# The last two key blocks of stick-breaking attention in three high-and-low passes, with norms written in place

## The chip, the cores and the metric

The kernel runs on one core of one Trainium2 chip. The metric is the device time of one execution in microseconds, as the median of several runs.

## What is computed

The reference is one hybrid decoder layer over 528 tokens (16 learned meta tokens and 512 of the sequence) of width 2048, in float32. The part that matters here is the attention of 8 heads of 128 columns:

```python
q = _rmsnorm(q.reshape(b, L, N_ATTN_HEADS, HEAD_DIM), g_q[l])
k = _rmsnorm(k.reshape(b, L, N_ATTN_HEADS, HEAD_DIM), g_k[l])
...
z = einsum('bqhd,bkhd->bhqk', q_blk, k_ctx) / math.sqrt(HEAD_DIM)
causal = kpos[None, :] < qpos[:, None]
log_beta = jax.nn.log_sigmoid(z)
log_keep = jnp.where(causal, jax.nn.log_sigmoid(-z), 0.0)
log_pass = lax.cumsum(log_keep, axis=3, reverse=True) - log_keep
w = jnp.where(causal, jnp.exp(log_beta + log_pass), 0.0)
o = jnp.einsum('bhqk,bkhd->bqhd', w, v_ctx)
```

Beside it runs a gated short convolution over 1024 channels; then come an output projection with a residual, and a SwiGLU feed-forward block of width 5632.

## The kernel before

Everything is held transposed: channels (or keys) on the 128 partitions, tokens along the free axis. A large product is done as *high and low parts in three passes*: an operand is split into a rounded part (type F32R) and the remainder, and the product is high x high + high x low + low x high, each a pass of TensorE with F32R operands. `split(hi, lo, src)` (L323) makes the parts: a copy on ACT for the high part and a subtraction on DVE for the low part. Weights are loaded by DMA, split the same way (`split_quad`, L195) two pieces ahead of their use, and fed to `product` (L319). A product in plain F32 is a single call, but the profile shows it as two weight loads and two matmuls.

The eight heads come one after another (`head`, L514). For each head three products over the 16 blocks of the input give k (`pk`), q (`pq`) and v (`pv`) in PSUM, in passes of 256 and 272 columns for k and v, and of 512 for q. The smaller steps of a head are hung into the products of the next: `after(n, work)` (L290) holds a step until n blocks of the running products have been issued, and the framework then orders the instructions of each engine once, when the program is built. Each engine runs its own instructions in that order and waits at semaphores.

The steps of a head are these:

- `read_qk` (L405) reads k or q out of PSUM into a temporary `raw`. `qk_norm` (L489) sums the squares over the partitions with a matrix of ones (`ss_k`, `ss_q`, L501 and L502) and normalises by `rsqrt` (L326). The result goes to a tile of its own, `kn` (640 columns, of which 528 are tokens and the rest zeros) or `qn` (512). Then the high and low parts are made: `kh`, `kl` of the first 384 columns of `kn`, and `qh`, `ql` of all of `qn`.
- `attend` (L542) transposes v into PSUM (`ta` for the first four blocks of 128 keys, `tb` for the last 16). The first 384 columns are split into `vh`, `vl`; the last two blocks are copied into `v32` in F32. There are five key blocks: four of 128 keys and one of 16. The queries that a block has to meet begin at `Q0 = [0, 112, 240, 368, 496]`, so the logits of the blocks are 512, 400, 272, 144 and 16 queries wide. Blocks 0, 1 and 2 are done in three passes (L561 to L563), blocks 3 and 4 in F32 (L565, L566), into the columns of block 2's tile, so that there are three segments of 512, 400 and 432 columns.
- Per segment, ACT and DVE form softplus and log-sigmoid (`sp`, `lb`, L587 to L591), POOL masks (`causal`, L573), and `split` makes parts for the reverse cumulative sum, which is a product with a triangular matrix (`sums`, L610; `c`, L615 to L621). Segments are chained by one carry row: L626 and the split behind it. `sums` then forms the weights and splits them into `wh`, `wl`: all columns of segments 0 and 1, and the first 272 of segment 2.
- `mix` (L640) adds up the output `o`: blocks 0 to 2 in three passes (L645 to L647), block 3 in F32 with 128 rows (L648), block 4 in F32 with 16 rows (L649). Then `o` is scaled, split and sent to DRAM.

PSUM holds four small tiles (`small`, L66) in rotation, which the transposes, the logits, the sums and the outputs share. The temporaries with tag `e` (two of them) hold `raw` of k, `raw` of q and v in turn.

Of the kernel before, what the change touches and what calls it, by code (L numbers as in the profile page):

```python
# [9 lines left out]
F32 = mybir.dt.float32  # L10
F32R = mybir.dt.float32r
# [22 lines left out]
def hybrid_layer(ctx: ExitStack, tc: tile.TileContext, xT, w_in, w_out, w_gu, w_down, vecs, out):  # L34
# [288 lines left out]
    def split(hi, lo, src, eng=ve):  # L323
        return sc.copy(hi, src), eng.tensor_tensor(lo, src, hi.bitcast(F32), ALU.subtract)  # L324

    def rsqrt(dst, v, n, y=None, t=None, eng=ve, times=None):  # L326

        y = t512(n, "r", 3) if y is None else y
        t = t512(n, "r", 3) if t is None else t
        sc.activation(y[:, :n], v, AF.Ln)  # L330
        sc.activation(y[:, :n], y[:, :n], AF.Exp, scale=-0.5)
        last = sc.activation(t[:, :n], y[:, :n], AF.Square)
        if times is not None:
            eng.tensor_tensor(y[:, :n], y[:, :n], times, ALU.mult)
        eng.scalar_tensor_tensor(t[:, :n], t[:, :n], -0.5, v, ALU.mult, ALU.mult)
        eng.scalar_tensor_tensor(dst, t[:, :n], 1.5, y[:, :n], ALU.add, ALU.mult)
        return last
# [105 lines left out]


    apool = open_pool("apool", side="right")
    kns = [apool.tile([P, 640], F32, name=f"kn{i}") for i in range(1)]
    for t in kns:
        gp.memset(t[:, L:640], 0.0)
    for tag, n in (("kh", 384), ("kl", 384), ("sh", L), ("sl", L), ("qn", SEQ), ("qh", SEQ), ("ql", SEQ), ("bh", 288), ("bl", 288), ("sp", 1344)):
        apool.tile([P, n], F32 if tag in ("qn", "sp") else F32R, tag=tag, name=f"first_{tag}")  # L450
    accp.tile([P, 48], F32, name="pad_acc")
    acc_c = accp.tile([P, SEQ], F32, name="acc_c")
    acc_a = accp.tile([P, SEQ], F32, name="acc_a")
# [32 lines left out]
            split(st[:, :, 0], st[:, :, 1], x[:, m : m + 2])  # L486
            gp.dma_start(mix_dram[:, 2 - m : 4 - m, k], st.rearrange("p a b n -> p a (b n)"))

    def qk_norm(read, dst, parts_of, name):  # L489

        raw, s, cols = read[:3]
        sh = apool.tile([P, L], F32R, tag="sh", name=f"sh_{name}")[:, :cols]
        sl = apool.tile([P, L], F32R, tag="sl", name=f"sl_{name}")[:, :cols]
        cuts = [(0, cols)] if cols == SEQ else [(0, T2), (T2, L)]
        split(sh, sl, s)

        def finish():
            v = t512(L, "v", 2)[:, :cols]
            for a, b in cuts:
                q = small(f"ss_{name}{a}")[:, : b - a]  # L500
                pe.matmul(q, ones_r, sh[:, a:b], start=True, stop=False)  # L501
                pe.matmul(q, ones_r, sl[:, a:b], start=False, stop=True)  # L502
                ve.scalar_tensor_tensor(
                    v[:, a:b], q, 1.0 / P, eps_r2[:, L - cols + a : L - cols + b], ALU.mult, ALU.add
                )
            rsqrt(dst, v, cols, times=raw)
            hi, lo, n = parts_of
            split(hi, lo, dst[:, :n])

        return finish  # L510

# [2 lines left out]
    def head(h):  # L514

        if h:
            pk = pp.tile([P, 2, 512], F32, tag="pp", name=f"pk{h}")
            product(parts_of_all(pk), n_hl)
        read = read_qk(flat(pk), g_k, L) if h else read_k0
        kn = kns[0]  # L520
        kh = apool.tile([P, 384], F32R, tag="kh", name=f"kh{h}")
        kl = apool.tile([P, 384], F32R, tag="kl", name=f"kl{h}")
        after(8 if h else 19, qk_norm(read, kn[:, :L], (kh, kl, 384), f"k{h}"))

        if h:
            load_mix(h - 1)
            pq = pp.tile([P, 2, 512], F32, tag="pp", name=f"pq{h}")
            product([(pq[:, 0, :], META, L)], n_hl)
        read = read_qk(pq[:, 0, :], gq_s, SEQ) if h else read_q0
        qn = apool.tile([P, SEQ], F32, tag="qn", name=f"qn{h}")  # L530
        qh = apool.tile([P, SEQ], F32R, tag="qh", name=f"qh{h}")
        ql = apool.tile([P, SEQ], F32R, tag="ql", name=f"ql{h}")
        after(9 if h else 22, qk_norm(read, qn, (qh, ql, SEQ), f"q{h}"))

        pv = pp.tile([P, 2, 512], F32, tag="pp", name=f"pv{h}")
        product(parts_of_all(pv), n_hl)
        vt = t512(L, "e", 2)
        with tc.high_priority(0 if h else 1 << 20):
            ve.tensor_tensor(vt[:, :L], flat(pv), r, ALU.mult)
        after(6 if h else 15, lambda: attend(h, kn, kh, kl, qn, qh, ql, vt))  # L540

    def attend(h, kn, kh, kl, qn, qh, ql, vt):  # L542

        ta, tb = small(f"va{h}"), small(f"vb{h}")
        for b in range(4):
            pe.transpose(ta[:, b * P : (b + 1) * P], vt[:, b * P : (b + 1) * P], ident)
        pe.transpose(tb[:16, :P], vt[:, 512:L], ident)
        vh = apool.tile([P, 384], F32R, tag="vh", name=f"vh{h}")
        vl = apool.tile([P, 384], F32R, tag="vl", name=f"vl{h}")
        v32 = apool.tile([P, 256], F32, tag="v32", name=f"v32{h}")  # L550
        split(vh, vl, ta[:, :384])
        ve.tensor_copy(v32[:, :P], ta[:, 384:512])
        ve.tensor_copy(v32[:16, P:], tb[:16, :P])


        zs = {}
        for b in (2, 1, 0):
            zs[b] = z = small(f"z{h}_{b}")
            kk, q0 = slice(b * P, (b + 1) * P), Q0[b]
            n = SEQ - q0  # L560
            pe.matmul(z[:, :n], kh[:, kk], qh[:, q0:], start=True, stop=False)  # L561
            pe.matmul(z[:, :n], kh[:, kk], ql[:, q0:], start=False, stop=False)
            pe.matmul(z[:, :n], kl[:, kk], qh[:, q0:], start=False, stop=True)  # L563
            if b == 2:
                pe.matmul(z[:, 272:416], kn[:, 384:512], qn[:, 368:], start=True, stop=True)  # L565
                pe.matmul(z[:, 416:432], kn[:, 512:640], qn[:, 496:], start=True, stop=True)  # L566


        lw = apool.tile([P, 1344], F32, tag="lw", name=f"lw{h}")
# [40 lines left out]
        def sums(s):  # L610
            a, b = SEG[s]
            th, tl = hl[s]
            c = small(f"c{h}_{s}")
            if s == 2:
                pe.matmul(c[:, :432], later_r, th, start=True, stop=False)  # L615
                pe.matmul(c[:, :432], later_r, tl, start=False, stop=False)
                pe.matmul(c[:, P:416], ones_r, bh, start=False, stop=False)
                pe.matmul(c[:, P:416], ones_r, bl, start=False, stop=True)
            else:
                pe.matmul(c[:, : b - a], carry, th, start=True, stop=False)  # L620
                pe.matmul(c[:, : b - a], carry, tl, start=False, stop=True)  # L621
            if s:

                n, (a0, b0) = SEQ - Q0[s], SEG[s - 1]
                th, tl = hl[s - 1]
                ve.tensor_tensor(lw[0:1, b0 - n : b0], c[0:1, :n], sp[0:1, a : a + n], ALU.add)  # L626
                split(th[0:1, :], tl[0:1, :], lw[0:1, a0:b0])
                after(6, lambda: sums(s - 1))
            ve.tensor_tensor(lb[:, a:b], lb[:, a:b], c[:, : b - a], ALU.subtract)
            sc.activation(lw[:, a:b], lb[:, a:b], AF.Exp)  # L630
            causal(lw, s)
            n = (512, 400, 272)[s]
            th = apool.tile([P, b - a], F32R, tag=f"th{s}", name=f"wh{h}_{s}")
            tl = apool.tile([P, b - a], F32R, tag=f"tl{s}", name=f"wl{h}_{s}")
            split(th[:, :n], tl[:, :n], lw[:, a : a + n])
            ws[s] = (th[:, :n], tl[:, :n])
            if s == 0:
                after(11, lambda: mix(ws))

        def mix(ws):  # L640
            o = small(f"o{h}")
            for b in range(3):
                kk, q0 = slice(b * P, (b + 1) * P), Q0[b]
                th, tl = ws[b]
                pe.matmul(o[:, q0:], vh[:, kk], th, start=b == 0, stop=False)  # L645
                pe.matmul(o[:, q0:], vh[:, kk], tl, start=False, stop=False)
                pe.matmul(o[:, q0:], vl[:, kk], th, start=False, stop=False)  # L647
            pe.matmul(o[:, Q0[3] :], v32[:, :P], lw[:, 1184:1328], start=False, stop=False)  # L648
            pe.matmul(o[:, Q0[4] :], v32[:16, P:], lw[:16, 1328:1344], start=False, stop=True)  # L649
            g = g_att[:, h : h + 1]  # L650
            st = stage(f"st_o{h}")[:, : 2 * SEQ].rearrange("p (a b) -> p a b", a=2)
            hi = sc.activation(st[:, 0], o, AF.Copy, scale=g)
            lo = ve.scalar_tensor_tensor(st[:, 1], o, g, st[:, 0].bitcast(F32), ALU.mult, ALU.subtract)
            square_sum(acc_a, o, h == 0, eng=ve)
            gp.dma_start(oa_dram[h], st)
            if h < HEADS - 1:
                with tc.issue_after(hi.ins), tc.issue_after(lo.ins):
                    mix_x(h)
# [592 lines left out]
```

## Time and profile before

| what | value |
|---|---|
| median of three runs | 2037.42 us (2037.31 to 2037.79) |
| profiled execution, its own time | 2037.97 us |
| its span, first to last instruction | 2036.1 us |
| granted TensorE clock | 1.000 |
| attention of the eight heads | about 56 to 373 us of the span |
| instructions | 39674 |

The span is what the profile's views cover; the execution's own time is 1.87 us longer. In the views, PE is TensorE's matmul and PEld its weight load, DVE is VectorE, ACT is ScalarE, POOL is GpSimd. A row of the timeline gives start, duration, engine, line, operation and tiles (out<-in), then partitions x columns and a count. A row of the waits gives the waiting instruction, what it waited for, and the total, number and longest of these waits.

### The profile page before, as it was taken

The numbers are of one execution on the slowest core, as the hardware profiler recorded it, in microseconds if no ns is written. First come the engines' busy times: TensorE is split into PE (matmuls) and PEld (weight loads), VectorE is DVE, ScalarE is ACT, GpSimd is POOL, SyncE is SP. The second block draws the span as 40 slices with busy tenths as digits, with TensorE's granted clock in tenths as the row PEclk, the third lists the DMA queues.
The fourth block names the chain that finished last, engine by engine and source line by source line (L and its number), as shares of the span: only waits on it lengthen the run. The fifth ranks groups of instructions, "written<-read, shape, count | busy, mean of one in ns | idle before, by whom it ended". The sixth has DMA issues, their size and how long they took to land.

```text
span 2036.1 us, 39674 instructions
## 1 busy us (share of the span) xinstructions
PE 2022.7 (99%) x16158; PEld 1962.6 (96%) x16158; DVE 1728.1 (85%) x2196; ACT 1078.8 (53%) x1556; POOL 337.9 (17%) x507
## 2 busy tenths in 40 slices
PE   9999999999999999999999999999999999999999
PEld 8999999899998889999999999999999999999999
DVE  7877777698878778998988988988998978888887
ACT  7776766344454445555555555555555544444443
POOL 0111111200014440111111110110110242131211
PEclk9999999999999999999999999999999999999999
DMA  6343344833355556556555555555555999797864
GB/s 221 102 140 123 125 136 136 270 104 107 104 205 175 167 160 203 146 171 181 149 168 160 152 168 157 154 168 156 158 166 153 283 340 349 170 313 200 220 151 89
DMA packets 156087, 356.30 MB, mean 175 GB/s; under 512 B 13632, under 2 KB 67648, under 8 KB 155136
## 3 DMA queue, kind: packets, MB, share of 16 engines
q1 hardware_dynamic: 72208, 216.76, 33.4%
q0 software_dynamic: 83696, 136.99, 25.1%
q8 instruction: 127, 2.08, 0.4%
q14 instruction: 56, 0.46, 0.1%
HBM read 275.78 MB, written 77.92 MB: 174 GB/s over the span
## 4 chain that ended last, share of the span: by engine, by line
PE 92%; DVE 3%; DMA 2%; ACT 1%; issue 1%; POOL 0%; SPq 0%; DVEq 0%; ACTq 0%; POOLq 0%
PE x L795 13%; PE x L797 13%; PE x L796 13%; PE z L795 7%; PE z L796 7%; PE z L797 7%; PE y L796 3%; PE y L797 3%; PE y L795 3%; PE pv L311 2%; PE pv L312 2%; PE pv L313 2%; PE pk L312 1%; PE pk L311 1%; PE pk L313 1%; PE pq L313 1%
## 5 line engine op out<-in xcount | busy, mean ns | idle before, releaser
L202 ACT CAST sw_split<-sw_in 128x1024 fp32r<-128x1024 f32 (+2 forms) x668 | 661.7, 992 | 709.8 <-PE z L796 193.3
L203 DVE TENSOR_TENSOR sw_split<-sw_in,sw_split 128x1024 fp32r<-128x1024 f32 (+2 forms) x668 | 777.8, 1165 | 149.2 <-ACT sw_split L202 144.3
L797 PE MATMUL x<-f,sw_split 128*128 128x256 f32 x1408 | 387.4, 275 | 0.4 <-DVE sw_split L203 0.4
L795 PE MATMUL x<-f,sw_split 128*128 128x256 f32 x1408 | 387.4, 275 | 0.1
L796 PE MATMUL x<-f,sw_split 128*128 128x256 f32 x1408 | 387.3, 275 | 0.0
L797 PEld LDWEIGHTS x<-f,sw_split 128*128 128x128 f32 x1408 | 264.3, 188 | 0.6 <-DVE sw_split L203 0.6
L795 PEld LDWEIGHTS x<-f,sw_split 128*128 128x128 f32 x1408 | 264.3, 188 | 0.5 <-ACT sides L811 0.5
L796 PEld LDWEIGHTS x<-f,sw_split 128*128 128x128 f32 x1408 | 264.3, 188 | 0.0
L1066 POOL DMA_DIRECT2D fd<-s x147 | 103.7, 922 | 710.8 <-DVE s L324 710.0
L209 DVE TENSOR_TENSOR sw_in<-sw_in 128x1024 f32<-128x1024 f32 (+1 forms) x164 | 187.9, 1146 | 13.1 <-DMA sw_in<-w_in 5.0
L797 PE MATMUL z<-f,sw_split 128*128 128x256 f32 x704 | 193.8, 275 | 1.7 <-DVE sw_split L203 1.7
L795 PE MATMUL z<-f,sw_split 128*128 128x256 f32 x704 | 193.9, 275 | 1.5 <-ACT sides L811 1.3
L796 PE MATMUL z<-f,sw_split 128*128 128x256 f32 x704 | 193.7, 275 | 0.0
L797 PE MATMUL x<-ring,sw_split 128*128 128x256 f32 x608 | 167.3, 275 | 0.5 <-DVE sw_split L203 0.5
L795 PE MATMUL x<-ring,sw_split 128*128 128x256 f32 x608 | 167.2, 275 | 0.0
L796 PE MATMUL x<-ring,sw_split 128*128 128x256 f32 x608 | 167.2, 275 | 0.0
L797 PEld LDWEIGHTS z<-f,sw_split 128*128 128x128 f32 x704 | 132.2, 188 | 1.9 <-DVE sw_split L203 1.9
L795 PEld LDWEIGHTS z<-f,sw_split 128*128 128x128 f32 x704 | 132.2, 188 | 1.9 <-ACT sides L811 1.5
L796 PEld LDWEIGHTS z<-f,sw_split 128*128 128x128 f32 x704 | 132.2, 188 | 0.0
L797 PEld LDWEIGHTS x<-ring,sw_split 128*128 128x128 f32 x608 | 114.1, 188 | 0.7 <-DVE sw_split L203 0.7
L795 PEld LDWEIGHTS x<-ring,sw_split 128*128 128x128 f32 x608 | 114.1, 188 | 0.0
L796 PEld LDWEIGHTS x<-ring,sw_split 128*128 128x128 f32 x608 | 114.1, 188 | 0.0
(609 smaller groups left out, 5459.1 us busy)
## 6 DMA issues: line engine op xcount, KB each, us to landing
sw_in<-w_gu SPq DMA_DIRECT2D x176, 512.0 KB, 4.0
sw_in<-w_in SPq DMA_DIRECT2D x92, 512.0 KB, 3.4
fd<-s POOLq DMA_DIRECT2D x147, 256.0 KB, 5.3
sw_in<-w_down SPq DMA_DIRECT2D x96, 384.0 KB, 4.3
ring<-fd POOLq DMA_DIRECT2D x42, 768.0 KB, 16.8
sw_in<-w_out SPq DMA_DIRECT2D x32, 512.0 KB, 3.4
out_T<-d POOLq DMA_DIRECT2D x54, 256.0 KB, 4.7
mix_dram<-st_x POOLq DMA_DIRECT2D x16, 516.0 KB, 4.1
```

The costliest lines, as they stand in the source:

```text
L202: sc.copy(hi, src)
L203: ve.tensor_tensor(lo, src, hi.bitcast(F32), ALU.subtract)
L209: return ve.tensor_tensor(sums[name], a, b, ALU.add)
L311: pe.matmul(ps, wh, ah[:, a:b], start=k + i == 0, stop=False)
L312: pe.matmul(ps, wh, al[:, a:b], start=False, stop=False)
L313: pe.matmul(ps, wl, ah[:, a:b], start=False, stop=k + i == last)
L795: pe.matmul(p, hi[:, kk], ah, start=start and j == k == 0, stop=False, skip_group_check=skip)
L796: pe.matmul(p, hi[:, kk], al, start=False, stop=False, skip_group_check=skip)
L797: pe.matmul(p, lo[:, kk], ah, start=False, stop=k == n - 1, skip_group_check=skip)
L1066: gp.dma_start(fd[c][s][:, :, k], t[:, :, i])
```

## The change

The keys get full-width parts: `kh` and `kl` are two fixed tiles of 640 columns whose last 112 are zeroed once, on DVE, instead of a memset of `kn` on POOL. `kn`, `qn` and `v32` go. The norms of k and q are written over `raw` and split from there, k over all 528 columns. v is split whole: 512 columns from `ta` and the 16 rows of `tb`. The logits of blocks 3 and 4 and their outputs are done in three passes each, like those of the other blocks, and the weights of segment 2 are split over all of its 432 columns.

```diff
-    kns = [apool.tile([P, 640], F32, name=f"kn{i}") for i in range(1)]
-    for t in kns:
-        gp.memset(t[:, L:640], 0.0)
-    for tag, n in (("kh", 384), ("kl", 384), ("sh", L), ("sl", L), ("qn", SEQ), ("qh", SEQ), ...
+    kh, kl = (apool.tile([P, 640], F32R, name=name) for name in ("kh", "kl"))
+    for t in (kh, kl):
+        ve.tensor_scalar(t[:, L:640], ones[:, : 640 - L], 0.0, None, ALU.mult)
+    for tag, n in (("sh", L), ("sl", L), ("qh", SEQ), ("ql", SEQ), ...
...
-            rsqrt(dst, v, cols, times=raw)
-            hi, lo, n = parts_of
-            split(hi, lo, dst[:, :n])
+            rsqrt(raw, v, cols, times=raw)
+            split(hi, lo, raw)
...
-        after(8 if h else 19, qk_norm(read, kn[:, :L], (kh, kl, 384), f"k{h}"))
+        after(8 if h else 19, qk_norm(read, kh[:, :L], kl[:, :L], f"k{h}"))
...
-        v32 = apool.tile([P, 256], F32, tag="v32", name=f"v32{h}")
-        split(vh, vl, ta[:, :384])
-        ve.tensor_copy(v32[:, :P], ta[:, 384:512])
-        ve.tensor_copy(v32[:16, P:], tb[:16, :P])
+        split(vh[:, :512], vl[:, :512], ta)
+        split(vh[:16, 512:], vl[:16, 512:], tb[:16, :P])
...
+        def logits(out, b):
+            kk, q0 = slice(b * P, (b + 1) * P), Q0[b]
+            pe.matmul(out, kh[:, kk], qh[:, q0:], start=True, stop=False)
+            pe.matmul(out, kh[:, kk], ql[:, q0:], start=False, stop=False)
+            pe.matmul(out, kl[:, kk], qh[:, q0:], start=False, stop=True)
...
-                pe.matmul(z[:, 272:416], kn[:, 384:512], qn[:, 368:], start=True, stop=True)
-                pe.matmul(z[:, 416:432], kn[:, 512:640], qn[:, 496:], start=True, stop=True)
+                logits(z[:, 272:416], 3)
+                logits(z[:, 416:432], 4)
...
-            n = (512, 400, 272)[s]
+            n = b - a
...
-            for b in range(3):
+            for b in range(5):
+                s, rows = min(b, 2), 16 if b == 4 else P
                 kk, q0 = slice(b * P, (b + 1) * P), Q0[b]
-                th, tl = ws[b]
-                pe.matmul(o[:, q0:], vh[:, kk], th, start=b == 0, stop=False)
-                pe.matmul(o[:, q0:], vh[:, kk], tl, start=False, stop=False)
-                pe.matmul(o[:, q0:], vl[:, kk], th, start=False, stop=False)
-            pe.matmul(o[:, Q0[3] :], v32[:, :P], lw[:, 1184:1328], start=False, stop=False)
-            pe.matmul(o[:, Q0[4] :], v32[:16, P:], lw[:16, 1328:1344], start=False, stop=True)
+                a = (0, 0, 0, 272, 416)[b]
+                th, tl = (t[:rows, a : a + SEQ - q0] for t in ws[s])
+                pe.matmul(o[:, q0:], vh[:rows, kk], th, start=b == 0, stop=False)
+                pe.matmul(o[:, q0:], vh[:rows, kk], tl, start=False, stop=False)
+                pe.matmul(o[:, q0:], vl[:rows, kk], th, start=False, stop=b == 4)
```

More of the change, by code (lines that the diff above doesn't have):

```diff
@@ L445, in hybrid_layer @@
     apool = open_pool("apool", side="right")
-    kns = [apool.tile([P, 640], F32, name=f"kn{i}") for i in range(1)]
-    for t in kns:
-        gp.memset(t[:, L:640], 0.0)
-    for tag, n in (("kh", 384), ("kl", 384), ("sh", L), ("sl", L), ("qn", SEQ), ("qh", SEQ), ("ql", SEQ), ("bh", 288), ("bl", 288), ("sp", 1344)):
-        apool.tile([P, n], F32 if tag in ("qn", "sp") else F32R, tag=tag, name=f"first_{tag}")
+    kh, kl = (apool.tile([P, 640], F32R, name=name) for name in ("kh", "kl"))
+    for t in (kh, kl):
+        ve.tensor_scalar(t[:, L:640], ones[:, : 640 - L], 0.0, None, ALU.mult)
+    for tag, n in (("sh", L), ("sl", L), ("qh", SEQ), ("ql", SEQ), ("bh", 288), ("bl", 288), ("sp", 1344)):
+        apool.tile([P, n], F32 if tag == "sp" else F32R, tag=tag, name=f"first_{tag}")
     accp.tile([P, 48], F32, name="pad_acc")
@@ L487, in mix_x, with qk_norm @@
             gp.dma_start(mix_dram[:, 2 - m : 4 - m, k], st.rearrange("p a b n -> p a (b n)"))
-    def qk_norm(read, dst, parts_of, name):
+    def qk_norm(read, hi, lo, name):
         raw, s, cols = read[:3]
@@ L519, in head @@
         read = read_qk(flat(pk), g_k, L) if h else read_k0
-        kn = kns[0]
-        kh = apool.tile([P, 384], F32R, tag="kh", name=f"kh{h}")
-        kl = apool.tile([P, 384], F32R, tag="kl", name=f"kl{h}")
-        after(8 if h else 19, qk_norm(read, kn[:, :L], (kh, kl, 384), f"k{h}"))
+        after(8 if h else 19, qk_norm(read, kh[:, :L], kl[:, :L], f"k{h}"))
         if h:
@@ L529, in head @@
         read = read_qk(pq[:, 0, :], gq_s, SEQ) if h else read_q0
-        qn = apool.tile([P, SEQ], F32, tag="qn", name=f"qn{h}")
         qh = apool.tile([P, SEQ], F32R, tag="qh", name=f"qh{h}")
         ql = apool.tile([P, SEQ], F32R, tag="ql", name=f"ql{h}")
-        after(9 if h else 22, qk_norm(read, qn, (qh, ql, SEQ), f"q{h}"))
+        after(9 if h else 22, qk_norm(read, qh, ql, f"q{h}"))
         pv = pp.tile([P, 2, 512], F32, tag="pp", name=f"pv{h}")
@@ L539, in head, with attend @@
             ve.tensor_tensor(vt[:, :L], flat(pv), r, ALU.mult)
-        after(6 if h else 15, lambda: attend(h, kn, kh, kl, qn, qh, ql, vt))
-    def attend(h, kn, kh, kl, qn, qh, ql, vt):
+        after(6 if h else 15, lambda: attend(h, qh, ql, vt))
+    def attend(h, qh, ql, vt):
         ta, tb = small(f"va{h}"), small(f"vb{h}")
@@ L547, in attend @@
         pe.transpose(tb[:16, :P], vt[:, 512:L], ident)
-        vh = apool.tile([P, 384], F32R, tag="vh", name=f"vh{h}")
-        vl = apool.tile([P, 384], F32R, tag="vl", name=f"vl{h}")
-        v32 = apool.tile([P, 256], F32, tag="v32", name=f"v32{h}")
-        split(vh, vl, ta[:, :384])
-        ve.tensor_copy(v32[:, :P], ta[:, 384:512])
-        ve.tensor_copy(v32[:16, P:], tb[:16, :P])
-        zs = {}
+        vh = apool.tile([P, 640], F32R, tag="vh", name=f"vh{h}")
+        vl = apool.tile([P, 640], F32R, tag="vl", name=f"vl{h}")
+        split(vh[:, :512], vl[:, :512], ta)
+        split(vh[:16, 512:], vl[:16, 512:], tb[:16, :P])
+        zs = {}
+        def logits(out, b):
[3 more added lines that the diff above has]
+            pe.matmul(out, kl[:, kk], qh[:, q0:], start=False, stop=True)
         for b in (2, 1, 0):
             zs[b] = z = small(f"z{h}_{b}")
[L559 to L563, printed above, removed]
+            logits(z[:, : SEQ - Q0[b]], b)
             if b == 2:
-                pe.matmul(z[:, 272:416], kn[:, 384:512], qn[:, 368:], start=True, stop=True)
-                pe.matmul(z[:, 416:432], kn[:, 512:640], qn[:, 496:], start=True, stop=True)
+                logits(z[:, 272:416], 3)
+                logits(z[:, 416:432], 4)
         lw = apool.tile([P, 1344], F32, tag="lw", name=f"lw{h}")
```

## The prediction

> **What bounds the kernel now.** I read the page first: span, engines, the chain.
>
> ```profile
> span 2036.1 us, 39674 instructions
> ...
> PE 2022.7 (99%) x16158; PEld 1962.6 (96%) x16158; DVE 1728.1 (85%) x2196; ACT 1078.8 (53%) x1556; POOL 337.9 (17%) x507
> ...
> PE 92%; DVE 3%; DMA 2%; ACT 1%; issue 1%; POOL 0%; SPq 0%; DVEq 0%; ACTq 0%; POOLq 0%
> ```
>
> TensorE is the bound over the whole span, and weight loads (PEld) are there nearly as often as matmuls (PE). The edits touch only the attention of the eight heads, so I took busy time by stage, one row per stretch: its length, then PE, PEld, DVE, ACT and POOL, then the granted clock. This is the row of head 2.
>
> ```profile
> 131.50:173.00 41.50, 41.50 (x287) 38.89 (x286) 31.30 (x55) 29.11 (x48) 5.60 (x16) 1.00 0.40 128
> ```
>
> The steady head takes 41.5 us; PE has no idle time in it at full clock, DVE is idle for 10.2 us and ACT for 12.4. Then the waits of the weight loads between 55 and 95 us, where head 0 is:
>
> ```profile
> PEld c L621 <- DVE spl L324: 0.5, 2, 0.3
> PEld z L562 <- DVE ql L324: 0.5, 1, 0.5
> PEld z L561 <- ACT qh L324: 0.4, 1, 0.4
> ```
>
> Head 0 is the one place where TensorE waits for the k, q and softmax work on ACT and DVE. The same view from 95 to 375 us has no row at all: in the other heads PE waits for nothing. So what counts is how much time the changed instructions take on PE, and what a longer ACT and DVE chain does in head 0.
>
> **How a matmul's slot is read.** These are weight loads (PEld) and matmuls (PE) of head 2 around the logits; the first three PE rows are ordinary passes of 272 and 512 columns.
>
> ```profile
> 101.25 0.28 PE L313 MATMUL pk<-n,sw_split 128*128 128x272 f32 x1
> 101.37 0.39 PE L311 MATMUL pq<-n,sw_split 128*128 128x512 f32 x1
> 101.60 0.39 PE L312 MATMUL pq<-n,sw_split 128*128 128x512 f32 x1
> ...
> 133.96 0.41 PE L565 MATMUL z<-qn,kn 128*128 128x144 f32 x2
> 134.21 0.29 PE L566 MATMUL z<-qn,kn 128*128 128x16 f32 x2
> ```
>
> ```profile
> 134.08 0.31 PEld L566 LDWEIGHTS z<-qn,kn 128*128 128x128 f32 x2
> 134.32 0.19 PEld L561 LDWEIGHTS z<-qh,kh 128*128 128x128 f32 x1
> 134.43 0.19 PEld L562 LDWEIGHTS z<-ql,kh 128*128 128x128 f32 x1
> ```
>
> Durations overlap; the distance between starts is the price. From start to start a pass of 272 columns takes 0.12 us and one of 512 takes 0.23: some 0.43 ns a column. A load starts when the matmul before its own starts to stream, so the load rows tell where a short matmul really stands. An fp32 product is two instructions: L565 (144 columns) runs from 133.96 to 134.21, 0.25 us for the product, 0.12 each. L566 (16 columns) has next to nothing to stream, yet from its first load (134.08) to the load that follows its second (134.32) pass 0.24 us: one slot is still L565's 0.12, the other is 0.11. That 0.11 us is the weight load itself. The next row, from 134.32 to 134.43, is again 0.11, and there it is a load of the high part kh behind a 16-column matmul. Head 0 shows a load of a high part with nothing beside it:
>
> ```profile
> 60.30 0.19 PEld L562 LDWEIGHTS z<-ql,kh 128*128 128x128 f32 x1 [0.47 <-DVE ql L324]
> 60.41 0.19 PEld L563 LDWEIGHTS z<-qh,kl 128*128 128x128 f32 x1
> ```
>
> The load that had waited for ql starts at 60.30, and its matmul lets the next load start at 60.41: 0.11 us once more. So a pass costs the larger of its columns and 0.11 us, and 0.11 us is what some 240 columns take. No high-and-low pass in this kernel is under 256 columns; the new ones have 144 and 16.
>
> **Logits, on the path.** Removed: the two fp32 products, from 133.96 to 134.43 (where the L561 behind them really starts), 0.47 us. Added: six passes. Three of 144 columns would stream in 144 x 0.43 = 62 ns and so take the load's 0.11; three of 16 take 0.11 too. 6 x 0.11 = 0.66; minus 0.47 is +0.19 us a head, +1.5 in eight.
>
> The row bounds the new passes from both sides. Below: columns only, 3 x 0.062 + 3 x 0.007 = 0.21, or -0.26 a head. Above: a narrow pass costs what a whole fp32 product costs, 0.25; 3 x 0.25 + 3 x 0.11 = 1.08, or +0.61. I take 0.11, because rows show it for these loads.
>
> The Trainium skill ("TensorE: Matmul & The Clock Gate", section "Back-to-back issue gap") has the gap of a warm matmul as N/2.4 + 2.5 ns, which is an estimate of 62 ns for 144 columns and a floor near 25 ns for 16; by that the six passes would take 0.26 us, 0.21 less than now. The trace's 16-column matmuls at 0.11 us do not agree: here the load sets the pace.
>
> **Outputs, on the path.** The same place for the weights times v, head 1:
>
> ```profile
> 124.30 0.41 PE L648 MATMUL o<-lw,v 128*128 128x144 f32 x2
> ```
>
> ```profile
> 124.63 0.29 PEld L649 LDWEIGHTS o<-lw,v 16*128 16x128 f32 x2
> 124.95 0.19 PEld L311 LDWEIGHTS pv<-n,sw_split 128*128 128x128 f32 x1
> 125.06 0.19 PEld L312 LDWEIGHTS pv<-n,sw_split 128*128 128x128 f32 x1
> ```
>
> L648's two end streaming at 124.30 + 2 x 0.12 = 124.54, but the load for the 16-row block starts only at 124.63: 0.09 us late, and then its 0.11 is bare. On the way out, from the second L649 (124.63 + 2 x 0.11 = 124.85) to the next load 0.10, and again 0.11 bare, until L311 starts at 125.06. Total 0.76. The change keeps both switches of row count and replaces 2 x 0.12 by 0.11 + 0.11 + 0.06 (the last of the three has no load beside it), and two 16-row passes by three: 0.28 + 0.09 + 0.11 + 0.11 + 0.11 + 0.10 + 0.11 = 0.91, +0.15 a head, +1.2 in eight. Bounds: below, columns only, -0.03 a head; above, 0.25 for each 144-column pass, +0.62.
>
> **ACT, DVE and POOL, off the path but for head 0.**
>
> ```profile
> L324 ACT CAST kh<-kn x6: 513/513/514, 114.0 to 321.4; 128x384 fp32r<-128x384 f32 x6
> ...
> L324 DVE TENSOR_TENSOR kl<-kn,kh x6: 557/560/560, 114.5 to 321.9; 128x384 fp32r<-128x384 f32 x6
> ...
> L324 ACT CAST sh_k<-tmp x6: 626/630/632, 104.5 to 311.6; 128x528 fp32r<-128x528 f32 x6
> ...
> L324 DVE TENSOR_TENSOR sl_k<-tmp,sh_k x6: 707/708/709, 105.1 to 312.3; 128x528 fp32r<-128x528 f32 x6
> ...
> L552 DVE COPY v<-va x7: 272/280/283, 93.6 to 342.5; 128x128 f32<-128x128 f32 x7
> ...
> L553 DVE COPY v<-vb x7: 269/269/272, 92.3 to 342.7; 16x128 f32<-16x128 f32 x7
> ```
>
> Splitting k over 528 columns instead of 384 costs what the sh_k and sl_k rows say: +0.12 on ACT, +0.15 on DVE. v's split from 384 to 512 columns I take at the same. The last weights' split grows from 272 to 432 columns, +0.13 and +0.15 by the same slope. The 16-row tail of v gets a cast on ACT and a subtraction on DVE; the nearest row is L553's 0.27, and DVE loses that copy and L552's 0.28. A head: ACT +0.64, DVE 0.45 - 0.28 = +0.17. Idle ACT (12.4 us) and DVE (10.2) hide it. The tightest of the hidden steps are two:
>
> ```profile
> 112.57 0.77 DVE L324 TENSOR_TENSOR spl<-lw,sph 1x512 fp32r<-1x512 f32 x1
> ...
> 128.51 0.68 DVE L324 TENSOR_TENSOR ql<-qn,qh 128x512 fp32r<-128x512 f32 x1
> ```
>
> ```profile
> 113.84 0.19 PEld L621 LDWEIGHTS c<-spl,carry 128*128 128x128 f32 x1
> ```
>
> The carry row is split by 113.34, and its load is issued at 113.84: 0.5 us of cover, from which the larger weights' split takes 0.28. ql is done at 129.2, over 4 us ahead of the logits' stretch. If the cover fails, a head loses what is short of it.
>
> Norms written over the tile read from PSUM take the same instruction and only hold that tile until the split, some 1.4 us longer (cast 0.62, subtraction 0.68); its next writer comes at least one product of 48 passes later, 5.8 us at 0.12 each. Nothing. The zeroed pad moves from POOL to two DVE instructions ahead of the first data: nothing. No DMA is added or moved.
>
> Head 0 has no cover. Its qh waits behind k's split, v's split and their casts on DVE: 0.12 + 0.15 + 0.15 = 0.42 at most, and the three stalls above turn that into PE time; the carry's second stall (0.3) can take the weights' 0.28 too. Between 0 and 0.7 I take 0.5, near the top, since these are stalls already.
>
> **Sum.** 1.5 + 1.2 + 0.5 = +3.2 us. The profiled execution took 2037.97 us with a span of 2036.1; the span should become 2039.3. The median of the runs is 2037.42, 0.55 under the profiled one, and the sum on it gives 2040.6 us, +0.16%. A measurement here tells 0.2%, 4.1 us, from no change.
>
> **Rivals.**
> *Narrow high-and-low passes run slowly.* If under 256 columns a pass costs as much as the fp32 product of that width, the upper bounds hold: 8 x (0.61 + 0.62) + 0.5 = +10.3, 2047.7 us, slower. For it: no such pass under 256 columns is in the trace, and 256 to 272 are the narrowest. Against: 256 to 512 columns follow one line, and the load alone explains why narrow ones gain nothing. It decides once a 144-column pass takes over about 0.16 us (with the switch at +0.2%). Chance 0.13.
> *A released buffer comes later.* The third logits tile z takes the PSUM buffer of the transposed v, which DVE now frees after a split of 512 columns instead of after a split and a copy. If PE stands for the extra 0.3 us in seven heads: 3.2 + 2.1 = +5.3, 2042.7, slower. Against: the copy that goes (0.28) pays for the larger split (0.15), and PE itself comes there 0.19 later. Chance 0.08.
> *Columns only.* If loads hid under one another: 8 x (-0.26 - 0.03) + 0.5 = -1.8, 2035.6, no change that can be told. That is the mechanism that the skill's gap formula stands for. Against: every load row above. Chance 0.05.
>
> **How the numbers follow.** The forecast has the other 0.74. Its own spread, some 1 us for head 0 and for a slightly different order of instructions, puts about a tenth of the whole above +4.1. Slower: 0.13 + 0.08 + 0.09 = 0.30. Faster by over 4.1 us needs columns only and some luck besides: 0.02. Same: 0.68. The range of 8 in 10 leaves out the slow passes and the columns-only case (0.18 together): 2038.1 to 2044.4. The low end lies half-way from the forecast to columns only; the high end is the buffer rival with the 0.5 us cover failing by 0.24 in seven heads besides.
>
> **What would show it.** Right: loads of the six logits passes 0.11 us apart, the stretch from the first of them to the next ordinary pass 0.66 us; the output's stretch 0.91; a steady head 0.34 longer; still no wait of a load in heads 1 to 7; the four waits of head 0 longer by about 0.5 in sum. Wrong: 144-column passes 0.25 apart (slow passes), or under 0.08 (columns only); new wait rows for z behind vl; a later stage that moves by over a microsecond, which nothing here foresees.

## The result and the profile after

The changed kernel takes 2041.2 us (median of 20 runs, 2040.49 to 2042.51), the kernel before 2037.38 us in runs beside it: +3.82 us, a ratio of 1.0019 with a 95% interval of 1.0012 to 1.0025. The forecast was 2040.6, in a range of 2038.1 to 2044.4. The profiled execution has a span of 2039.6 us, 3.5 more than before. So the total came out close. It does not test the terms, though: the interval is +2.4 to +5.1 us, and the stages below show that head 0 cost three times what the forecast had for it.

The page after, span, engines and chain:

```profile
span 2039.6 us, 39729 instructions
...
PE 2025.2 (99%) x16190; PEld 1965.7 (96%) x16190; DVE 1730.1 (85%) x2190; ACT 1082.0 (53%) x1564; POOL 337.8 (17%) x506
...
PE 94%; DVE 3%; ACT 1%; DMA 1%; issue 1%; POOL 0%; SPq 0%; DVEq 0%; ACTq 0%; POOLq 0%
```

TensorE has 32 more matmuls, two in each of 16 places, and is still the bound. Weight loads of head 1's outputs after the change, with block 3 from the second row and block 4 from the fifth (lines have moved: L643 to L645 are the three passes):

```profile
126.47 0.19 PEld L645 LDWEIGHTS o<-wh,vl 128*128 128x128 f32 x1
126.59 0.19 PEld L643 LDWEIGHTS o<-wh,vh 128*128 128x128 f32 x1
126.72 0.19 PEld L644 LDWEIGHTS o<-wl,vh 128*128 128x128 f32 x1
126.83 0.19 PEld L645 LDWEIGHTS o<-wh,vl 128*128 128x128 f32 x1
127.10 0.18 PEld L643 LDWEIGHTS o<-wh,vh 16*128 16x128 f32 x1
127.20 0.18 PEld L644 LDWEIGHTS o<-wl,vh 16*128 16x128 f32 x1
127.31 0.19 PEld L645 LDWEIGHTS o<-wh,vl 16*128 16x128 f32 x1
127.52 0.19 PEld L311 LDWEIGHTS pv<-n,sw_split 128*128 128x128 f32 x1
127.63 0.19 PEld L312 LDWEIGHTS pv<-n,sw_split 128*128 128x128 f32 x1
```

Block 3's first matmul starts when the second load of the group does, at 126.72, and the ordinary product at 127.63: 0.91 us, where it was 0.76. The 144-column passes and the 16-column ones stand 0.11 apart, and both switches of row count are still there (126.83 to 127.10 and 127.31 to 127.52). The logits' stretch measures 0.667 us in the same way, before 0.467.

A steady head, from the first load of one head's outputs (heads 4 and 5) to that of the next. First the kernel before:

```profile
247.27 0.19 PEld L645 LDWEIGHTS o<-wh,vh 128*128 128x128 f32 x1
...
288.83 0.19 PEld L645 LDWEIGHTS o<-wh,vh 128*128 128x128 f32 x1
```

And after:

```profile
250.80 0.19 PEld L643 LDWEIGHTS o<-wh,vh 128*128 128x128 f32 x1
...
292.73 0.19 PEld L643 LDWEIGHTS o<-wh,vh 128*128 128x128 f32 x1
```

41.56 became 41.93, +0.37. What waits a weight load had between 40 and 105 us after the change (before, these were the three that the prediction shows and one of 0.5 for the low part of q's squares):

```profile
PEld va L541 <- issue: 1.0, 1, 1.0
PEld c L616 <- ACT sph L324: 1.0, 1, 1.0
PEld ss_q L502 <- DVE sl_q L324: 0.7, 2, 0.5
PEld z L553 <- DVE vl L324: 0.3, 1, 0.3
PEld c L617 <- DVE spl L324: 0.2, 1, 0.2
```

Two waits of a microsecond are new, both around head 0, and one of 0.3 stands in head 1's logits. The two waits of head 0's logits for `qh` and `ql`, 0.77 us of stall before the change, are gone. "issue" means that the view names no releaser; the transposes (L541) read the scaled v, which DVE finishes at 56.91, and their load starts at 57.03. From 105 to 385 us there is no wait.

To compare kernels, a *stall* below is what lies between two load starts beyond the larger of the columns' time and 0.11 us, where that is over 0.04 us. It is worked out from the starts of all loads. "Early" sums it from 40 to 94 us of the span without head 0's own switch of rows, "late" from 385 us on. Span, head and stalls come from one profiled execution of each kernel. The last two rows are the kernel before with passes appended behind 2030 us: up to there they run the same instructions, so they show how much one kernel differs from itself.

| kernel | median, us (against before beside it) | span | steady head | early | late |
|---|---|---|---|---|---|
| before | 2037.38 | 2036.1 | 41.57 | 1.88 | 10.6 |
| changed | 2041.2 (+3.8) | 2039.6 | 41.94 | 3.55 | 9.3 |
| outputs_only | 2039.5 (+2.0) | 2037.0 | 41.78 | 3.52 | 9.2 |
| logits_only | 2038.83 (+1.3) | 2037.0 | 41.77 | 2.20 | 9.1 |
| before_128_rows | 2035.18 (-2.3) | 2033.8 | 41.38 | 1.91 | 10.5 |
| after_128_rows | 2039.52 (+2.0) | 2038.4 | 41.69 | 3.80 | 9.8 |
| after_head0_later | 2040.97 (+3.8) | 2038.2 | 41.93 | 3.40 | 8.9 |
| after_three_buffers | 2040.39 (+3.4) | 2038.4 | 41.80 | 3.75 | 9.1 |
| q_in_place_only | 2037.21 (+0.1) | 2035.5 | 41.57 | 1.87 | 10.3 |
| best_later_steps | 2035.41 (-1.7) | 2033.7 | 41.38 | 1.90 | 10.7 |
| before_delay_3us | 2039.52 (+2.3) | 2037.4 | 41.57 | 1.92 | 9.3 |
| before_delay_1us | 2037.79 (+0.6) | 2036.2 | 41.57 | 1.90 | 9.5 |
| narrow_passes (to 2029 us) | | | 41.57 | 1.82 | 9.5 |
| narrow_passes_warm (to 2029 us) | | | 41.57 | 1.90 | 10.0 |

### The profile page after: what moved, and what is told of

It is laid out like the page before. It is cut to its first block, busy times and chain, and to the rows that moved or that the text cites. A ratio compares the mean times of both kernels' runs of the same rounds, so it can differ in the third digit from the quotient of the medians.

```text
span 2039.6 us, 39729 instructions
## 1 busy us (share of the span) xinstructions
PE 2025.2 (99%) x16190; PEld 1965.7 (96%) x16190; DVE 1730.1 (85%) x2190; ACT 1082.0 (53%) x1564; POOL 337.8 (17%) x506
## 4 chain that ended last, share of the span: by engine, by line
PE 94%; DVE 3%; ACT 1%; DMA 1%; issue 1%; POOL 0%; SPq 0%; DVEq 0%; ACTq 0%; POOLq 0%
PE x L793 13%; PE x L792 13%; PE x L791 13%; PE z L792 7%; PE z L791 7%; PE z L793 7%; PE y L792 3%; PE y L793 3%; PE y L791 3%; PE pq L311 1%; PE pq L312 1%; PE pq L313 1%; PE pv L311 1%; PE pv L312 1%; PE pv L313 1%; PE pk L312 1%
```

## The experiments

### The two halves by themselves

`outputs_only` is the kernel before with these edits:

```diff
-        split(vh, vl, ta[:, :384])
-        ve.tensor_copy(v32[:, :P], ta[:, 384:512])
-        ve.tensor_copy(v32[:16, P:], tb[:16, :P])
+        split(vh[:, :512], vl[:, :512], ta)
+        split(vh[:16, 512:], vl[:16, 512:], tb[:16, :P])
...
-            n = (512, 400, 272)[s]
+            n = b - a
...
+            for b in range(5):
...
```

The rest of `mix` is as in the change.

> Only the outputs' half of the change: v split whole, segment 2's weights split whole, blocks 3 and 4 of the outputs in three passes; logits and norms as before. Theory (a pass costs the larger of its columns and a weight load of 0.11 us): the output stretch of a head goes from 0.76 to 0.91 us, the eight heads together +1.2 us; logits stretch unchanged at 0.47; head 0's stalls within 0.3 us of before, so about +1.2 to +1.5 us in all. Rival (head 0's new order of instructions is most of the loss, the passes are nearly free): under +0.4 us. Rival (narrow passes are slow): +5 us.

Measured: ratio 1.0010 (1.0001 to 1.0019), +2.0 us. The stretch is 0.910 us in place of 0.761, the 0.15 of the theory, and the narrow passes are not slow. But the head grew by 0.21, since the third logits tile now waits 0.06 for its PSUM buffer, and head 0 stalls for 1.6 us more: the expectation had 0.3 at most, and +1.5 us in all.

`logits_only` is the changed kernel with v, the weights' split and `mix` as before.

> Only the logits' half: norms of k and q in place, k split whole, blocks 3 and 4 of the logits in three passes; v32 and the F32 outputs as before. Theory: the logits stretch goes from 0.47 to 0.66 us a head, +1.5 us in the eight heads, and head 0 waits longer because k's split is longer: +0.3 to +1.5 us more. In all +1.8 to +3. If the stall of the v transposes in head 0 (1.0 us after the change) belongs to this half, it is here and not in the run with the outputs alone. Rival (the parts add up with nothing left over): this and the outputs-only run sum to the whole +3.8 us; where they sum to clearly less, a part of the loss comes only from both together.

Measured: ratio 1.0007 (0.9998 to 1.0016), +1.3 us; by its interval alone this is not told from no change. It is less than the +1.8 to +3 that were expected. The stretch went from 0.467 to 0.667, the head from 41.57 to 41.77, exactly that. The stall ahead of the transposes of v, 1.03 us, is here and not in the other half; but the logits' two waits for q are gone here, and head 0's stalls are only 0.3 us more in sum. Waits of the two kernels, 40 to 95 us, outputs first:

```profile
PEld c L619 <- DVE spl L324: 1.3, 2, 1.1
PEld ss_q L502 <- DVE sl_q L324: 1.1, 2, 0.5
...
```

```profile
PEld va L541 <- issue: 1.0, 1, 1.0
PEld ss_q L502 <- DVE sl_q L324: 0.4, 1, 0.4
```

So each half brings one of the two new waits of a microsecond: the logits' half the one at the transposes, the outputs' half the one at the carry `c`. The traces show where the outputs' wait comes from. These are the cast of segment 2's weights on ACT and the cast of the next carry row, first in the kernel before:

```profile
75.72 0.42 ACT L324 CAST wh<-lw 128x272 fp32r<-128x272 f32 x1 [0.72 <-POOL lw L578]
...
77.73 0.62 ACT L324 CAST sph<-lw 1x512 fp32r<-1x512 f32 x1
```

And in the changed kernel, with two of the DVE rows between them:

```profile
76.93 0.56 ACT L324 CAST wh<-lw 128x432 fp32r<-128x432 f32 x1 [1.97 <-POOL lw L574]
77.52 0.61 DVE L324 TENSOR_TENSOR wl<-lw,wh 128x432 fp32r<-128x432 f32 x1 [0.69 <-ACT wh L324]
...
79.84 0.56 DVE L622 TENSOR_TENSOR lw<-c,sp 1x400 f32<-1x400 f32 x1
80.43 0.62 ACT L324 CAST sph<-lw 1x512 fp32r<-1x512 f32 x1 [0.37 <-DVE lw L622]
```

POOL masks segment 2 in three pieces (`causal`): columns 0 to 128, 272 to 400 and 416 to 432. A split of the first 272 columns needs only the first piece, and in the kernel before the cast starts 0.04 us after that one ends (75.68). A split of all 432 columns needs all three, and in the changed kernel the cast starts 0.04 us after the third ends (76.89). So ACT stands 1.97 us in place of 0.72, in `outputs_only` 1.98, and what ACT and DVE do behind it comes later: the parts of q, of k and of the carry row, for which TensorE then waits. In all kernels of the table that split 432 columns ACT waits 1.28 to 1.98 us at this place, in those that split 272 it waits 0.15 to 0.72. No run changes this split alone.

The medians of the halves add up to +3.3 beside +3.8 for the whole; the intervals do not separate these. The spans do not add up (+0.9 each, +3.5 together); they are of one execution each, and the last experiment shows that such spans differ by about a microsecond without any change.

### The switch of rows

`before_128_rows`:

```diff
+    v32 = apool.tile([P, 256], F32, name="v32")
+    gp.memset(v32[:, P:], 0.0)
...
-            pe.matmul(o[:, Q0[4] :], v32[:16, P:], lw[:16, 1328:1344], start=False, stop=True)
+            pe.matmul(o[:, Q0[4] :], v32[:, P:], lw[:, 1328:1344], start=False, stop=True)
```

> The kernel before, with the 16-key block of the outputs done over all 128 rows: v32 is one fixed tile whose rows 16 to 127 of the last block are zero, and the masked weights there are zero as well. Theory (switching the number of rows leaves a weight load bare on the way in and on the way out): L648 to the next product shrinks from 0.76 to 4 slots of 0.12, 0.12, 0.11, 0.11 = 0.46 us, -0.30 a head, -2.4 us in all. Rival (the gap is the semaphore wait that L649 carries, not the rows): nothing changes, within 0.3 us of before.

Measured: ratio 0.9987 (0.9979 to 0.9996), -2.3 us. Loads of head 1's outputs in this kernel (L649 is block 3, L650 block 4):

```profile
123.27 0.31 PEld L649 LDWEIGHTS o<-lw,v 128*128 128x128 f32 x2
123.52 0.31 PEld L650 LDWEIGHTS o<-lw,v 128*128 128x128 f32 x2
123.75 0.19 PEld L311 LDWEIGHTS pv<-n,sw_split 128*128 128x128 f32 x1
123.86 0.19 PEld L312 LDWEIGHTS pv<-n,sw_split 128*128 128x128 f32 x1
```

No gap is left: the stretch is 0.464 us (0.46 expected), 0.30 less than with 16 rows, although the load of block 4 still waits for its semaphore. So the gaps came from the row count. The head gained only 0.19, as the third logits tile then waits 0.11 for the transposed v to be read by DVE. No kernel of the study is faster.

`after_128_rows` does the same to the changed kernel (`vh`, `vl` fixed, the last block zeroed once, `rows = P`).

> The changed kernel, with its 16-key output passes over all 128 rows (vh and vl fixed, last block zeroed once). Theory: six slots of 0.11 = 0.66 us instead of 0.91, -0.25 a head, -2.0 us against the changed kernel, so about +1.8 us against before. Rival (semaphore, not rows): no different from the changed kernel, +3.8 us.

Measured: 0.666 us for the stretch, six slots of 0.11; the head is 0.25 shorter than the changed kernel's 41.94, and the kernel takes 2.0 us more than before (1.8 expected). With the switch gone from both, three passes still cost 0.20 more than the F32 products.

### Head 0

`after_head0_later` hangs head 0's attention three blocks later: `after(6 if h else 18, ...)` in place of 15.

> The changed kernel, with the attention of head 0 (transposes of v and logits) hung three blocks later into the next head's products (18 instead of 15). Theory (head 0's loss is a place in the order: the transposes stand on PE where DVE has not yet scaled v, 1.04 us): that stall goes, and the carry's stall of 1.05 us stays or shrinks; span 1.0 to 2.0 us under the changed kernel's. Rival (the longer splits of k and v are a delay that PE pays wherever the steps stand): the stall turns up again at the logits or the carry, gain under 0.4 us.

Measured: +3.8 us against before, as the changed kernel. The theory fell: the transposes moved, and the stall did not. It is now at the q product, and it ends with the same DVE instruction. The span is 1.4 us shorter, but this execution was 0.76 us ahead before any step that moved: its load for the low part of q's squares stands at 47.75 us, that of the changed kernel at 48.51. DVE and weight loads of this kernel:

```profile
54.23 0.71 DVE L324 TENSOR_TENSOR kl<-tmp,kh 128x528 fp32r<-128x528 f32 x1 [0.70 <-ACT kh L324]
54.85 0.69 DVE L334 TENSOR_TENSOR tmp<-tmp,tmp 128x512 f32<-128x512 f32 x1
55.46 0.70 DVE L534 TENSOR_TENSOR tmp<-pv,r 128x528 f32<-128x528 f32 x1
```

```profile
55.12 0.19 PEld L313 LDWEIGHTS pk<-n,sw_split 128*128 128x128 f32 x1
56.27 0.19 PEld L311 LDWEIGHTS pq<-n,sw_split 128*128 128x128 f32 x1 [0.97 <-PE pk L313]
```

L534 scales v out of PSUM and ends at 56.16; the product of the next q, which takes the PSUM buffer that v leaves, goes on at 56.27. And L534 stands behind k's split. In the kernel before, the same instruction (L539) ran at 52.59, ahead of k's norm being written:

```profile
51.97 0.70 DVE L335 SCALAR_TENSOR_TENSOR tmp<-tmp,tmp 128x528 f32<-128x528 f32 x1
52.59 0.70 DVE L539 TENSOR_TENSOR tmp<-pv,r 128x528 f32<-128x528 f32 x1
```

The scaled v takes the temporary that held raw k. Written in place, that temporary is in use until k is split. `after_three_buffers` gives the tag three temporaries (`t512(L, "e", 3)` at its three uses) and changes nothing else.

> The changed kernel with three temporaries instead of two under the tag of raw k, raw q and scaled v. Theory (a norm written in place holds raw k until its split, and in head 0 the scaled v, which takes the same buffer, must wait for that; until then the PSUM bank of v, which the next q product needs, is not free): DVE scales v in head 0 before k's norm, near 48.5 us instead of 56.2, and the PE stall of 1.04 us there is gone; head 0 comes 1.0 us or more earlier to its first output and the span is 0.8 to 1.5 us under the changed kernel's 2039.6. Rival (the place in DVE's order comes from the larger splits, not from the buffer): v stays behind k's split and nothing is gained.

DVE in this kernel:

```profile
47.17 1.12 DVE L324 TENSOR_TENSOR sl_q<-tmp,sh_q 128x512 fp32r<-128x512 f32 x1
48.21 0.69 DVE L534 TENSOR_TENSOR tmp<-pv,r 128x528 f32<-128x528 f32 x1
```

v is scaled at 48.21, 8 us earlier than in the changed kernel (56.21), and the stall of 1.04 is gone: the mechanism holds. The gain does not: +3.4 us against before, by intervals not told from the changed kernel, and head 0's first output comes 0.27 us earlier (88.97 for 89.24) where 1.0 was expected. The early stalls are 3.75 us in sum, now at the logits (0.62 for qh) and at the sums (0.86 and 0.65). So head 0 waits for its chain on ACT and DVE, and removing one wait uncovers the next: of this the rival in the experiment before was right. `best_three_buffers`, the kernel before with three temporaries and the 128 rows, was not measured: it leaves 2.97 KB a partition for a pool that needs 4.03.

`q_in_place_only` is the kernel before with `qn = read[0]`, so that q's norm alone is written in place.

> The kernel before, where only q's norm is written over what was read from PSUM (no qn tile); k, v, logits and outputs as before. Theory: nothing to pay, steady heads 41.57 us as before, time within 0.5 us of before. Rival (holding the temporary longer delays its next writer): a steady head longer by 0.05 us or more, or a new wait of a read of PSUM.

Measured: ratio 1.0000 (0.9991 to 1.0010), head 41.57, early stalls as before. The next writer of raw q's buffer does come late, and for q writing in place costs nothing. In-place writing of k alone was not run.

`best_later_steps` is before_128_rows with head 0's norm of q at block 24 (22) and its attention at 17 (15).

> The kernel before with its 16-key output block over 128 rows, and with head 0's steps later: the norm of q at block 24 instead of 22, its attention at 17 instead of 15. Theory (head 0's five stalls, 1.9 us in sum, are places in the order): at least 1 us of them goes, span near 2032.5 us against 2033.8 with the old places. Rival (they turn up behind other steps): span 2033.8 as with the old places.

Measured: -1.7 us against before, no gain over before_128_rows (span 2033.7 against 2033.8). The wait for q's squares went, and the wait of the logits for qh grew from 0.34 to 0.95: the rival. Moving steps of head 0 about has not paid in either attempt.

### The narrow pass by itself

`narrow_passes` appends sets of 16 high-part matmuls, and of 8 F32 products, to the kernel before, behind its last product.

> The kernel before with a row of matmuls behind its last product: high-part passes of 16, 64, 144, 208, 256 and 400 columns, 16 of each, then F32 products of 16, 64 and 144 columns, 8 of each; nothing else is changed. Theory (larger of columns and weight load): the high-part passes start 0.11 us apart at 16, 64, 144 and 208 columns, 0.117 at 256 and 0.18 at 400; an F32 product costs 0.22 at 16 and 64 columns and 0.25 at 144. Rival (slow under 256 columns): 0.25 at 144, 0.36 at 208. Rival (columns only): 0.03 at 64, 0.07 at 144, 0.10 at 208.

Measured: 0.112 us at 16 columns and for the first six at 64, but 0.213 at 144 and 208. Neither theory said so. The granted clock, the third number from the right, explains it (two stretches of this kernel):

```profile
2030.50:2032.50 2.00, 2.00 (x21) 2.00 (x19) 0.85 (x2) 0.00 (x0) 0.00 (x0) 1.00 0.02 7
2033.00:2036.00 3.00, 3.00 (x16) 3.00 (x16) 0.00 (x0) 0.00 (x0) 0.00 (x0) 0.51 0.05 20
```

After 2.5 us of narrow passes the clock fell to a half, and a load took twice as long. At the end of the sets, back at full clock, 256 columns took 0.117 to 0.121 and 400 took 0.180. `narrow_passes_warm` holds the clock with 24 passes of 512 columns ahead of each set.

> The kernel before with matmuls behind its last product: 24 passes of 512 columns ahead of each set, to hold the clock, then 8 high-part passes of 16, 64, 144 and 208 columns, then 4 F32 products of 16, 64 and 144 columns. Theory (a pass costs the larger of its columns and a load of 256 clocks): 0.107 to 0.112 us for 16, 64, 144 and 208 columns at full clock, 0.11 for each half of an F32 product at 16 and 64 columns and 0.12 at 144. Rival (narrow high-part passes are slow by width): 0.25 at 144, 0.36 at 208.

Measured at a clock of 1.00: 0.108 to 0.112 us at 16, 64, 144 and 208 columns alike; each half of an F32 product 0.111 at 16 and 64 columns, 0.122 at 144. The set of eight at 144 columns:

```profile
2048.57 1.01 PE L1198 MATMUL bench<-sw_split 128*128 128x144 f32 x8
2049.42 0.67 PE L1193 MATMUL bench<-sw_split 128*128 128x512 f32 x2
```

From 2048.57 to 2049.42 lie eight slots, 0.106 each by these rows of matmuls; the loads themselves start 0.108 to 0.112 apart. Width does not matter up to 208 columns. The Trainium skill ("TensorE: Matmul & The Clock Gate", section "Back-to-back issue gap") gives its formula, an estimate of 62 ns for 144 columns, for an isolated matmul and without the load. Here every pass has its own load, and the slot was 0.11 us.

### What the later stages take back

`before_delay_3us` is the kernel before with TensorE time added and nothing else, `before_delay_1us` the same with 6 passes:

```diff
+            for _ in range(13 if h == 3 and b == 0 else 0):
+                pe.matmul(z[:, :n], kh[:, kk], qh[:, q0:], start=True, stop=True)
```

> The kernel before with 13 repeated passes of 512 columns ahead of the last logits tile of head 3 (the same product again, overwritten): 13 x 0.227 = 2.95 us of TensorE time and nothing else. It asks why the stages behind the attention have 1.3 us less stall in the changed kernel. Theory (they absorb part of any delay, since some of their waits end at times that TensorE does not set): first output of head 7 later by 2.95 us, stalls behind 385 us shorter by about 1.3 us, span up by about 1.7 us. Rival (it comes from what the change does to tiles and splits): stalls behind 385 us as before within 0.3 us, span up by 2.9 us.

> The same with 6 passes, 6 x 0.227 = 1.36 us. Theory (absorbed): the stalls behind 385 us shrink by up to 1.3 us and the span moves by 0.1 to 1.0 us. Rival: span up by 1.3 us, stalls as before within 0.3 us.

Measured: the longer delay lengthens one head by 3.02 us and the span by 1.3, and the late stalls fall from 10.6 to 9.3; the shorter lengthens it by 1.40, the span by 0.1, with late stalls of 9.5. This looks like the theory, but the table's last two rows take the ground from it: without any delay the same kernel has late stalls of 9.5 and 10.0. From head 7's first output load to the last product the kernel before took 1660.6 us, with the delays 1659.2 and 1659.5, and with passes appended only behind that 1659.4 and 1659.9. The executions also start differently: before reaches head 0's outputs 0.37 and 0.15 us later than the two with a delay. The medians grow by 2.3 and 0.6, with intervals of 1.0000 to 1.0018 and 0.9994 to 1.0011, which hold the full 3.0 and 1.4 us. So neither the theory nor the rival is decided, and it is not shown that later stages take anything back.

The order of instructions behind 385 us is the same on every engine before and after the change. What sets the late waits was not traced.

## Why the prediction was right, and where it was not

- **Logits, +0.19 a head: right.** 0.467 became 0.667, +0.20. The pass costs the weight load, at every width tried up to 208 columns.
- **Outputs, +0.15 a head: right.** 0.761 became 0.910. The two switches of row count cost what the reading of the rows said, and taking them out gave 0.30 a head in the stretch. The two terms together are 8 x 0.349 = 2.8 us, as forecast.
- **ACT and DVE, nothing outside head 0: right for heads 2 to 7.** The carry's cover of 0.5 us and that of ql held, with no wait from 105 us on.
- **Head 0, +0.5 within 0 to 0.7: wrong, 1.67 us** (early stalls 1.88 to 3.55). The step that failed is "The last weights' split grows from 272 to 432 columns, +0.13 and +0.15": it has the longer split and not what the split waits for. The cast needs all three masks in place of one and waits 1.97 us where it waited 0.72. With the outputs' half alone head 0 stalls 1.64 us more.
- **Norms in place, "Nothing": wrong in head 0, but cheap.** "Its next writer comes at least one product of 48 passes later" holds for q and for steady heads. In head 0 k's norm comes late, behind the place of the scaled v, and that v is the next writer. This brought 1.04 us, with a PSUM buffer as the link to TensorE in `after_head0_later`. But the logits' waits for `qh` and `ql` (0.77), which the prediction had growing, are gone with it. The logits' half alone stalls only 0.32 us more, and the third temporary, which removes the 1.04, brings waits at the logits back.
- **The buffer rival (0.08): it happened, small.** 0.33 us in head 1, some 0.02 a head afterwards, not 0.3 in each.
- **Slow narrow passes (0.13) and columns only (0.05): neither.** 0.11 us at full clock, at every width from 16 to 208.
- **A slip of no consequence:** the prediction's "over about 0.16 us" for slow passes does not follow from its sum. The 0.9 us from 3.2 to 4.1 are reached by 48 passes of 144 columns at about 0.13 us each.

The span adds up so: 2.8 for the passes, 1.7 for head 0, 0.33 for head 1, 0.15 in small waits of the other heads, less 0.13 for an earlier start of this execution and 1.3 fewer stalls behind 385 us: 3.5. The forecast of 3.2 had 1.2 too little in head 0 and nothing for head 1. The last 1.3 are no effect of the change that the runs show, since the kernel before differs from itself by over a microsecond there (10.6 against 9.5). So the closeness of the total is in part luck: the attention by itself came out at +4.7 (head 7's first output load stands at 375.49 us where it was 370.83), and the medians' interval holds this as well as 3.2.

## What to carry to other kernels

Count a matmul as the larger of its columns and its weight load: splitting one narrow F32 product (two loads) into three passes (three loads) loses as soon as the load is the longer, and zeroed rows that keep the row count the same are cheaper than a smaller block (0.30 us in each place here). When a step is widened, look up what its new columns wait for, and not only how much longer it takes: here a longer wait for a mask cost more than the longer split. Before writing over a temporary, look up who takes that buffer next at the one place where the schedule is not yet steady. And before a difference between two traces is called an effect, compare the same stretch in two traces of the same code.

## What the runs showed of the hardware

- A load of 128 columns of these 4-byte weights takes 0.107 to 0.112 us at full clock and 0.213 at half clock, so it goes by TensorE's clock.
- Narrow passes without a gap lowered the granted clock from 1.00 to 0.5 after 2.5 us (16 of 16 columns and 6 of 64), though PE and its loads were never idle by their records. It came back 10 us later, in the set of 256 columns, and fell again in the F32 products of 64 columns. In the attention six narrow passes last 0.67 us, and the clock stayed at 1.00. The Trainium skill ("TensorE: Matmul & The Clock Gate", section "What's actually happening") lets the clock follow how busy the array has lately been; the runs agree, and suggest that a slot filled by a weight load does not count in full.
- A load for 16 rows behind a matmul of 128 rows does not start under it: in the kernel before it comes 0.09 us late and is bare for 0.11, and the way back costs 0.10 and 0.11. With 128 rows in its place the stretch is 0.30 us shorter. Loads that keep the row count start with the matmul ahead of theirs (a load at 124.18 and the matmul before its own at 124.17).
